# A 3x3 convolution whose output images are stored by even and by odd partitions: 32 transfers for 24

## The chip, the core and the metric

The kernel runs on one core of one Trainium2 chip. A core has five engines, each with its own instruction stream: TensorE (PE in the profile, with its weight loads as PEld), VectorE (DVE), ScalarE (ACT), GpSimd (POOL) and SyncE (SP), which here only issues DMA transfers. Sixteen DMA engines move data between the chip's memory (HBM) and the core's working memory (SBUF, 128 partitions); PSUM is the memory that TensorE writes to. The metric is the time of one execution in microseconds of device time. The kernel before takes 127.18 us, the median of three runs from 127.08 to 127.49.

## The reference

The computation is a 3x3 convolution with a border of zeros. Sixteen images of 64 channels and 64x64 points become sixteen images of 128 channels and 64x64 points, all in fp32:

```python
batch, c_in, h, w, c_out = 16, 64, 64, 64, 128
x_pad = np.pad(x, ((0, 0), (0, 0), (1, 1), (1, 1)), mode='constant')
for b in range(batch):
    for co in range(c_out):
        for ci in range(c_in):
            for kh in range(3):
                for kw in range(3):
                    output[b, co] += weight[co, ci, kh, kw] * x_pad[b, ci, kh:kh+h, kw:kw+w]
```

The input is 16.8 MB and the output 33.6 MB. Each output channel of an image is a row of 16 KB (64x64 fp32 numbers), and one image is 128 such rows, 2 MB.

## The kernel before, in words

The kernel uses a Winograd form of the convolution along the image rows: pairs of output rows are made from sums and differences of input rows, so that fewer matrix products are needed.

**Tiling.** Images go through in pairs. The 64 input channels of the first image of a pair lie on partitions 0 to 63 and those of the second on partitions 64 to 127, so one load of a pair is 128 partitions by 16 KB, 2 MB. There are eight pairs `p`, and each is worked in two halves `h` of 32 rows, so sixteen steps `(p, h)`. In a step, GpSimd makes sums, differences and outer differences of the rows in fp16 (lines 114, 121 and 127) two steps ahead, ScalarE makes an fp16 copy of 17 rows (line 132), TensorE runs 54 matrix products (line 170) into eight PSUM tiles, ScalarE copies six of them out (line 192), and VectorE (lines 247, 249, 251) and ScalarE (line 253) put the output rows together in fp32 in SBUF. In the output tiles the partition is the output channel, and every partition holds that channel's 16 KB row.

**Where the data live.** Large SBUF buffers are used more than once. Slots 0 to 4 of 16 KB for each partition, a double slot `two` for loads of pairs 3, 4, 6 and 7, and a double slot `b` for the outputs of pairs 0, 3 and 6 are handed round by the lists `X_HOME` and `O_HOME`. A tile's next user waits until the transfer that empties it has landed.

**Transfers.** All transfers are issued by SyncE, in one queue, in the order of the program. The weights and pairs 0 to 4 are loaded at the start; the loads of pairs 5, 6 and 7 follow after steps (1, 1), (3, 0) and (4, 0) (`NEXT_LOADS`, issued at line 67). Outputs of a pair are stored after its second half, by `store`. Pairs 0, 3 and 6 (`BOTH`) lie in the double slot and are stored by one transfer of 4 MB each (line 207). The other five pairs lie in two separate slots and are stored image by image (line 216). Image 11 (pair 5, second image, `FEW`) is stored in three transfers: 57 rows of all channels, then the last seven rows of 124 channels, then those of the last four channels. That makes 9 loads and 15 stores, 24 transfers.

**Completion semaphores.** The framework gives the transfers eight completion semaphores in turn. When transfer number n takes the semaphore that number n - 8 used, SyncE first waits until that earlier transfer has landed, unless something else has already made sure of it. This wait sits in SyncE's own queue, ahead of everything that SyncE issues later.

**Order.** `keep` holds the instructions of each engine in the order in which the program gives them, so nothing is rearranged by a scheduler.

Of the kernel before, what the change touches and what calls it, by code (L numbers as in the profile page):

```python
# [15 lines left out]
def kernel(  # L16
# [12 lines left out]
    nc = tc.nc  # L29
    B, CI, H, W = x.shape  # L30
    CO = weight.shape[0]
# [4 lines left out]
    keep = tc.keep_in_program_order  # L36
# [15 lines left out]
    FEW = 5, 1, 7  # L52
# [145 lines left out]
    def outputs(p):  # L198
        if O_HOME[p] == "b":
            both = slots.tile([128, 2, H, W], F32, tag="b", name="both")  # L200
            return both, [both[:, b2, :, :] for b2 in range(2)]
        return None, [home(k, "ot") for k in O_HOME[p]]

    def store(p, both, ots):
        if p in BOTH:
            pair = out[2 * p : 2 * p + 2, :, :, :].rearrange("b c h w -> c b h w")
            keep(nc.sync.dma_start(pair, both))
            return
        for b2 in range(2):
            parts = [(0, CO, 0, H)]  # L210
            if (p, b2) == FEW[:2]:
                at = H - FEW[2]
                parts = [(0, CO, 0, at), (0, 124, at, H), (124, 4, at, H)]
            for c, n, lo, hi in parts:
                keep(
                    nc.sync.dma_start(
                        out[2 * p + b2, c : c + n, lo:hi, :], ots[b2][c : c + n, lo:hi, :]
                    )
                )

    for n, (p, h) in enumerate(halves):
        if n + 2 < len(halves):
            tr[halves[n + 2]] = transforms(nc.gpsimd, *halves[n + 2])
        if h == 0:
            both, ots = outputs(p)
# [28 lines left out]
        if h == 1:  # L254
            store(p, both, ots)
# [32 lines left out]
```

## Time and profile before

| What | Value |
|---|---|
| Median of three runs | 127.18 us (127.08 to 127.49) |
| The profiled execution's own time | 127.13 us |
| Its span (first to last instruction) | 125.4 us |
| PE, DVE, ACT, POOL busy | 95.6, 66.8, 85.4, 90.5 us |
| Last output tile made by VectorE | 103.12 us |
| DMA: packets, bytes, mean rate | 3827, 50.78 MB, 405 GB/s |
| Share of the 16 DMA engines' time that is taken | 96.2% |
| Mean granted TensorE clock | 0.917 |

The profile is one execution, taken by the hardware profiler. Times in it count from the span's start. "Busy" is the time in which an engine executed something; waiting, branching and the issuing of transfers do not count. The DMA row of the page gives, for 40 equal slices of the span (3.1 us each), the mean busy share of the sixteen DMA engines in tenths, and the row below it what they moved in GB/s. Beside the views, the trace holds one record for each DMA packet: when it started, how long it took and how many bytes it moved. Data packets are mostly of 16,384 bytes, one channel's row; a packet of 4 bytes at the end of each transfer on each DMA engine is the write to the completion semaphore. The records do not name the DMA engine, but packets of one engine follow each other without a gap, so that each engine's series can be pieced together from starts and durations.

### The profile page before, as it was taken

The numbers are of one execution on the slowest core, as the hardware profiler recorded it, in microseconds if no ns is written. First come the engines' busy times: TensorE is split into PE (matmuls) and PEld (weight loads), VectorE is DVE, ScalarE is ACT, GpSimd is POOL, SyncE is SP. The second block draws the span as 40 slices with busy tenths as digits, with TensorE's granted clock in tenths as the row PEclk, the third lists the DMA queues.
The fourth block names the chain that finished last, engine by engine and source line by source line (L and its number), as shares of the span: only waits on it lengthen the run. The fifth ranks groups of instructions, "written<-read, shape, count | busy, mean of one in ns | idle before, by whom it ended". The sixth has DMA issues, their size and how long they took to land.

```text
span 125.4 us, 2343 instructions
## 1 busy us (share of the span) xinstructions
PE 95.6 (76%) x873; PEld 48.9 (39%) x873; DVE 66.8 (53%) x104; ACT 85.4 (68%) x150; POOL 90.5 (72%) x52
## 2 busy tenths in 40 slices
PE   0349999999999999999999999999999960000000
PEld 0223555555455555555555555555555520000000
DVE  0199658393939476574939394765749390000000
ACT  4458598989797988989897979789898930000000
POOL 2209999999999999999999999999999300000000
PEclk9999999999999999999999999999999996555555
DMA  4999999999999999999999999999999999999971
GB/s 132 371 453 423 434 424 439 423 335 418 434 431 429 426 434 418 423 429 434 416 439 424 423 423 423 418 431 434 423 424 423 433 416 443 423 429 444 418 335 47
DMA packets 3827, 50.78 MB, mean 405 GB/s; under 512 B 360, under 2 KB 488, under 8 KB 744
## 3 DMA queue, kind: packets, MB, share of 16 engines
q1 hardware_dynamic: 3816, 50.63, 96.2%
q8 instruction: 7, 0.11, 0.3%
q14 instruction: 4, 0.03, 0.1%
HBM read 17.07 MB, written 33.55 MB: 404 GB/s over the span
## 4 chain that ended last, share of the span: by engine, by line
PE 76%; DMA 2%; DVE 2%; POOL 1%; DVEq 0%; ACT 0%; issue 0%
PE acc L170 75%; DMA w_raw<-in_weight_dram 2%; DVE ss L114 1%; DVE ot L251 1%; POOL w L87 1%; DVEq L283 0%; DVE th L141 0%; DVE Wt L142 0%; PE wp L102 0%; ACT g0h L139 0%; DVEq L142 0%
## 5 line engine op out<-in xcount | busy, mean ns | idle before, releaser
L170 PEld LDWEIGHTS <-Wt 64*128 64x128 f16 x864 | 48.0, 96 | 48.5 <-issue 3.0
L192 ACT COPY ut<-acc 128x512 f32<-128x512 f32 x96 | 48.7, 612 | 4.4 <-PE acc L170 4.4
L170 PE MATMUL acc<-xh,Wt 64*128 64x504 f16 (+3 forms) x384 | 46.2, 372 | 0.0
L170 PE MATMUL acc<-ss,Wt 64*128 64x504 f16 (+1 forms) x192 | 24.8, 392 | 2.3 <-DVE ss L114 2.3
L170 PE MATMUL acc<-ee,Wt 64*128 64x504 f16 (+1 forms) x192 | 26.4, 377 | 0.0
L247 DVE TENSOR_TENSOR ot<-acc,ut 128x512 f32<-128x512 f32 x20 | 12.9, 686 | 20.0 <-ACT ut L192 15.8
L114 POOL TENSOR_TENSOR ss<-xs 128x1024 f16<-128x1024 f32 x7 | 16.6, 2366 | 4.7 <-DMA xs<-in_x_dram 4.7
L127 POOL TENSOR_TENSOR ee<-two 128x1024 f16<-128x1024 f32 x8 | 19.0, 2378 | 0.0
L114 POOL TENSOR_TENSOR ss<-two 128x1024 f16<-128x1024 f32 x8 | 19.0, 2369 | 0.0
L127 POOL TENSOR_TENSOR ee<-xs 128x1024 f16<-128x1024 f32 x7 | 16.6, 2376 | 0.0
L253 ACT COPY ot<-acc 128x512 f32<-128x512 f32 x20 | 10.7, 589 | 5.5 <-PE acc L170 5.5
L170 PE MATMUL acc<-dd,Wt 64*128 64x504 f16 (+1 forms) x96 | 13.9, 392 | 0.0
L247 DVE TENSOR_TENSOR both<-acc,ut 128x512 f32<-128x512 f32 x12 | 7.7, 686 | 11.0 <-ACT ut L192 7.9
L251 DVE TENSOR_TENSOR ot<-ut,acc 128x512 f32<-128x512 f32 x20 | 12.8, 682 | 0.2
L249 DVE TENSOR_TENSOR ot<-acc,ut 128x512 f32<-128x512 f32 x20 | 12.8, 680 | 0.0
L121 POOL TENSOR_TENSOR dd<-two 128x512 f16<-128x512 f32 x8 | 10.3, 1287 | 0.0
L121 POOL TENSOR_TENSOR dd<-xs 128x512 f16<-128x512 f32 x7 | 10.0, 1423 | 0.0
L132 ACT CAST xh<-two 128x1088 f16<-128x1088 f32 x8 | 9.3, 1157 | 0.0
L132 ACT CAST xh<-xs 128x1088 f16<-128x1088 f32 x8 | 9.2, 1145 | 0.0
L253 ACT COPY both<-acc 128x512 f32<-128x512 f32 x12 | 6.4, 589 | 3.5 <-PE acc L170 3.5
L251 DVE TENSOR_TENSOR both<-ut,acc 128x512 f32<-128x512 f32 x12 | 7.7, 683 | 0.1
L249 DVE TENSOR_TENSOR both<-acc,ut 128x512 f32<-128x512 f32 x12 | 7.7, 680 | 0.0
(23 smaller groups left out, 14.9 us busy)
## 6 DMA issues: line engine op xcount, KB each, us to landing
out_dram<-ot SPq DMA_DIRECT2D x9, 2048.0 KB, 18.5
out_dram<-both SPq DMA_DIRECT2D x3, 4096.0 KB, 22.5
xs<-in_x_dram SPq DMA_DIRECT2D x3, 2048.0 KB, 16.2
two<-in_x_dram SPq DMA_DIRECT2D x1, 4096.0 KB, 28.4
two<-in_x_dram SPq DMA_DIRECT2D x2, 2048.0 KB, 23.1
out_dram<-ot SPq DMA_DIRECT2D x1, 1824.0 KB, 24.3
xs<-in_x_dram SPq DMA_DIRECT2D x1, 1088.0 KB, 5.4
xs<-in_x_dram SPq DMA_DIRECT2D x1, 960.0 KB, 7.4
```

Source lines behind the costliest of these rows:

```text
L87: keep(nc.gpsimd.tensor_copy(w16[:, 0, :], w_raw))
L114: keep(eng.tensor_add(t, v[:, j : j + 16, 0, :], v[:, j : j + 16, 1, :]))
L121: keep(eng.tensor_sub(t, v[:, j : j + RB, 1, :], v[:, j : j + RB, 0, :]))
L127: keep(eng.tensor_sub(t, xs[p][:, r - 1 : r + 15, :], xs[p][:, r + 1 : r + 17, :]))
L132: keep(nc.scalar.copy(t, xs[p][:, C_ROW[h] : C_ROW[h] + 17, :]))
L170: nc.tensor.matmul(tiles[b2][:, lo:hi, c_lo:c_hi], Wt[p0 : p0 + 64, wi, kw, :], src[p0 : p0 + 64, first : last + 1 : step, c_lo + kw - 1 : ...
L192: keep(nc.scalar.copy(ut, tiles[b2]))
L247: keep(nc.vector.tensor_add(ov[b2][:, jg : jg + RB, 1, :], pg2[b2], ug[b2]))
L249: keep(nc.vector.tensor_add(ov[b2][:, jf : jf + RB, 0, :], pf1[b2], uy[b2]))
L251: keep(nc.vector.tensor_sub(ov[b2][:, jf : jf + RB, 1, :], ux[b2], pf2[b2]))
L253: keep(nc.scalar.copy(ov[b2][:, jg : jg + RB, 0, :], pg1[b2]))
```

## The change

Eight images that were stored by one transfer each are now stored by two: one takes the 64 even partitions (channels 0, 2, 4, ...), the other the 64 odd ones. The rows of 16 KB stay whole, so the number of rows and bytes moved is the same. The eight are both images of pairs 1, 2 and 4 and the first images of pairs 5 and 7. The second image of pair 5 (`FEW`) keeps its three transfers, and the second image of pair 7, the last transfer of the kernel, stays whole. Pairs 0, 3 and 6 are untouched. There are now 23 stores and 32 transfers. Line 216 of the kernel before becomes line 218. On the other engines nothing moves: the four compute engines have the same instructions in the same order.

```diff
         for b2 in range(2):
-            parts = [(0, CO, 0, H)]
+            image = out[2 * p + b2, :, :, :]
+            parts = [(slice(0, CO, 2), 0, H), (slice(1, CO, 2), 0, H)]
             if (p, b2) == FEW[:2]:
                 at = H - FEW[2]
-                parts = [(0, CO, 0, at), (0, 124, at, H), (124, 4, at, H)]
-            for c, n, lo, hi in parts:
-                keep(
-                    nc.sync.dma_start(
-                        out[2 * p + b2, c : c + n, lo:hi, :], ots[b2][c : c + n, lo:hi, :]
-                    )
-                )
+                parts = [(slice(0, CO), 0, at), (slice(0, 124), at, H), (slice(124, CO), at, H)]
+            elif p >= FEW[0] and b2 == 1:
+                parts = [(slice(0, CO), 0, H)]
+            for c, lo, hi in parts:
+                keep(nc.sync.dma_start(image[c, lo:hi, :], ots[b2][c, lo:hi, :]))
```

With the semaphores in turn, transfer n of the changed kernel waits for its own n - 8, so the pairing of transfers changes as well.

## The prediction

> **What bounds the kernel now.** I read the page from the top, then the windows of the last 25 us, then the transfers.
>
> ```profile
> PE   0349999999999999999999999999999960000000
> POOL 2209999999999999999999999999999300000000
> DMA  4999999999999999999999999999999999999971
> GB/s 132 371 453 423 434 424 439 423 335 418 434 431 429 426 434 418 423 429 434 416 439 424 423 423 423 418 431 434 423 424 423 433 416 443 423 429 444 418 335 47
> q1 hardware_dynamic: 3816, 50.63, 96.2%
> ```
>
> TensorE is full until slice 33 and then idle; the DMA engines are full from slice 2 to slice 38. The end of the time is set by transfers alone. The windows show it more closely (columns: length, busy time of PE, PEld, DVE, ACT, POOL, then clock, DMA share, GB/s):
>
> ```profile
> 90.00:100.00 10.00, 10.00 (x98) 5.14 (x94) 5.93 (x11) 8.84 (x17) 8.28 (x5) 1.00 1.00 427
> 104.00:110.00 6.00, 0.00 (x0) 0.00 (x0) 0.00 (x0) 0.00 (x0) 0.00 (x0) 0.55 1.01 431
> 110.00:120.00 10.00, 0.00 (x0) 0.00 (x0) 0.00 (x0) 0.00 (x0) 0.00 (x0) 0.50 1.01 433
> 120.00:122.00 2.00, 0.00 (x0) 0.00 (x0) 0.00 (x0) 0.00 (x0) 0.00 (x0) 0.50 0.71 303
> 122.00:124.00 2.00, 0.00 (x0) 0.00 (x0) 0.00 (x0) 0.00 (x0) 0.00 (x0) 0.50 0.21 90
> ```
>
> After 104 us no engine computes and DMA goes on at 431 to 433 GB/s; the share falls only from 120 us, when the sixteen DMA engines run out one by one. The chain of waits ends with VectorE at 103.12 us and then a wait of the closing line, so it does not name the transfers; the windows do. How far SyncE is ahead is read from the stores' view, and the tightest readers of landed data from the timelines of VectorE and GpSimd:
>
> ```profile
> DMA to landing us min/median/max: 12.0/20.6/26.6
> 82.71 1.29 DVE L247 TENSOR_TENSOR both<-acc,ut 128x512 f32<-128x512 f32 x2 [2.01 <-PE acc L170]
> 86.46 2.38 POOL L114 TENSOR_TENSOR ss<-two 128x1024 f16<-128x1024 f32 x1
> ```
>
> A 2 MB transfer takes 4.86 us of all DMA engines, so a store that lands 20.6 us after its issue stood behind some three others. The DMA queue is never short of work after 3 us. From the packet records: a 16,384-byte packet takes 611 ns and the next starts 607 ns after it, 16 x 16,384 bytes / 607 ns = 432 GB/s, the rate of the windows. The span (125.4) ends 0.83 us after the last landing at 124.52; the profiled run's own time is 127.13, so 1.73 us lie around the span, and it stands 0.05 us below the median of 127.18.
>
> **The change, part by part.**
>
> *Bytes and rows.* The same 128 rows of 16 KB for an image: no packet is cut, so nothing here at 611 ns each.
>
> *Eight more completion writes on each DMA engine.* In the records the write takes 9 ns, and a transfer of 8 packets on one engine takes 4.862 us against 8 x 607 ns = 4.856: 6 ns for the end of a transfer, no gap before the next one. The 4 MB stores say the same (9.719 us for 16 packets: 9.712 + 7). 8 x 6 ns = **0.05 us**, on the path. The Trainium skill ("DMA: Bandwidth & Descriptors", Anatomy of one DMA) gives a fixed cost of about 2 us for a transfer, mostly the wait for the write's receipt; were it paid in the queue, eight more would be an estimated 16 us. That page also says the cost can overlap, and the 6 ns here show that in this queue it does.
>
> *Eight more issues on SyncE.* An issue takes 332 to 1268 ns (median 356, stores of line 216), so 8 x 0.36 = 2.8 us, at most 10 us, over the whole run, and about 0.4 to 2.5 us at any one pair. What covers it: the data of the first split stores (issued from 34.1 us) start moving when the 4 MB store ahead of them ends, at 38.0 on the earliest DMA engine, and later ones have 5 us and more. At the end, pair 7 is issued from 103.18 in three pieces instead of two; its data start at 110.4 on the earliest engine, 7 us later. Were that cover gone, an issue would cost its own 0.36 us once for each. **0**, bounds 0 and +0.5.
>
> *Eight semaphores in turn.* Transfer n waits for n - 8, and there are now more, shorter transfers in between. I paired each with the landing of before (halves at 2.43 us). Numbering from 0, with stores ready when VectorE ended before: the load of pair 6 (number 16, ready 51.3) needs a half landed at 46.1; the 4 MB store of pair 3 (17, 57.8) needs 48.6; the load of pair 7 (18, 63.1) needs 51.0; pair 4's (19 to 22, from 68.7) need 55.8 to 63.2; pair 5's first image (23, 24, from 80.2) 65.6 and 71.5. All in time. Image 11 is the exception: its 57 rows (25) need the store of pair 3, landed at 81.28, and its seven rows (26) the load of pair 7, landed at 86.14, its last four channels (27) an even half due at about 88.6. Before, these were issued at 80.8 to 82.8; now SyncE is held until about 88.7. Queued behind it is only the 4 MB store of pair 6, ready at 92.27. And the DMA engines have work until 101.0 at the earliest (end of the 57 rows on the earliest engine), so 12 us remain. **0**; it would cost from a hold past 101 on.
>
> *Who waits for the landings.* VectorE rewrites the double slot at 82.71 and needs the store of pair 3 landed at 81.28 (1.4 us spare); GpSimd reads pair 7 at 86.46, landed at 86.14 (0.3 us spare). Both landings come after six to eight added completion writes, +0.03 to 0.04 us: still covered. If it were not, TensorE would stop, but the last stores may be issued 7 us later before DMA runs dry. **0**.
>
> *How 64 partitions are spread over the DMA engines.* This is not in the trace of before: all large transfers have 128 partitions. If each engine gets four rows of each half, its load is unchanged, but it may read partitions that another engine is reading at the same time. The nearest row is image 11's seven rows: 124 channels were moved by four DMA engines only (their completion arrives in four late steps, 103.42 to 104.19, after an early jump at issue), 31 packets of 1,792 bytes each, over all partitions that the other twelve were reading as well. All 124 took 74 ns. 1,792, 14,592 and 16,384 bytes in 74, 545 and 611 ns lie on one line (8 ns and 27.2 GB/s), and the twelve others lost nothing in these 2.2 us, bar one packet of +0.4 us beside an instruction fetch, and the disturbed engine named next, which was no slower than at other times. So **0** is nearest. Bounds: below, -0.8 (next part); above, what the one disturbed DMA engine shows: while stores ran beside computing, some 80 of its packets took about 653 instead of 611 ns; on every engine that is 8 images x 8 packets x 42 ns = +2.7 us.
> The Trainium skill ("SBUF — State Buffer", Door 1: The DMA port swizzle) has sixteen ports of about 27 GB/s, each serving eight partitions; two DMA engines on one port would get half each. The packets of 74 ns speak against it, since two engines together took some 51 GB/s there.
>
> **Sum:** 127.18 + 0.05 = 127.23, **127.2 us**. In the profile: last landing at about 124.57.
>
> **The rivals.**
>
> *Half speed (slower).* Two DMA engines share an SBUF port, or 64 partitions are given to eight engines only. Then each of the eight images takes 4.86 us more: +38.9, 166 us. For: four-engine transfers exist here, so the number of engines hangs on the shape. Against: the 74 ns packets, and 64 has room for sixteen equal shares. It decides as soon as an engine's packets in a split store take over 611 ns. Chance 0.08. Its mild form, 653 ns, gives 129.9: 0.12.
>
> *The stalls are drawn anew (slower).* The end is the latest of the sixteen DMA engines' series of packets, pieced together from the records: their last completion writes start at 124.16, 124.06, 123.37 and so on down to 120.17, mean 122.1. The latest lost 2.5 us at the first switch from loads to stores (26 to 29 us, slice 9 at 335 GB/s) and 1.1 us at 65 to 70 us, beside the load of pair 6. Single stalls of 0.35 to 0.47 us fall on other engines with instruction fetches. One more on the latest engine gives +0.4 to +0.9: 127.6 to 128.1. Chance 0.15; the runs of before, all within 0.41 us, speak against more.
>
> *The late engines are relieved (faster).* If the slow packets belong to certain partitions and not to the DMA engine, a new spread of partitions shares them out; or the 65 to 70 us stalls fall elsewhere. Then the third, 123.37, sets the end: -0.8, 126.4 us; even sharing, 122.1, would give -2.0. For: the slow series is slow in stores beside computing and clean in the loads, which looks like a path, not an engine at fault. Against: both late engines must be relieved at once. Chance 0.25.
>
> **How the numbers follow.** 0.3% (0.38 us) is about what a measurement can tell from no change. No change, 126.8 to 127.6: 0.40. Faster 0.25. Slower 0.15 + 0.12 + 0.08 = 0.35. The likeliest gives 127.2; its own range is 126.8 to 127.6. The range that leaves out no more than 2 in 10 goes from 126.2 to 129.9 and omits half speed and a gain of over 1 us.
>
> **What would show it.** Right: DMA share 9 in slices 2 to 38, 427 to 433 GB/s in the windows, the queue's share near 96%, SyncE held about 6 us longer at line 218 near 82 to 89 us, the 4 MB store of pair 6 issued near 92.3 still, no new wait of GpSimd or VectorE on a landing. Wrong: GB/s below 420 between 40 and 100 us (ports or engines shared), packets of 16,384 bytes well over 611 ns, a GpSimd wait for `two`, or a last landing below 123.8.

## The result and the profile after

The changed kernel takes 127.55 us (median of 20 runs, 127.33 to 128.29) against 127.14 us (20 runs, 126.75 to 127.66): a ratio of 1.0034, 95% interval 1.0021 to 1.0047. That is 0.41 us more, and it is just past the 0.3% that I had called the limit of what can be told.

The profiled execution took 127.45 us with a span of 125.3 us. The page after, with the lines that answer to those shown of before:

```profile
PE   0349999999999999999999999999999980000000
POOL 2209999999999999999999999999999400000000
DMA  4999999999999999999999999999999999999971
GB/s 112 392 438 434 424 455 424 418 345 418 429 434 421 431 439 413 397 424 445 421 429 413 424 434 424 434 424 431 424 424 430 410 444 427 434 424 434 439 335 58
q1 hardware_dynamic: 3944, 50.63, 96.3%
```

The DMA row is the same digit for digit, the same 50.63 MB are moved, and 128 packets more are counted: eight transfers by sixteen completion writes. The windows of the changed kernel (same columns as before):

```profile
90.00:100.00 10.00, 10.00 (x96) 5.10 (x94) 6.44 (x11) 8.68 (x17) 8.44 (x5) 1.00 1.01 429
104.00:110.00 6.00, 0.00 (x0) 0.00 (x0) 0.31 (x1) 0.00 (x0) 0.00 (x0) 0.64 0.99 423
110.00:120.00 10.00, 0.00 (x0) 0.00 (x0) 0.00 (x0) 0.00 (x0) 0.00 (x0) 0.50 1.01 433
120.00:122.00 2.00, 0.00 (x0) 0.00 (x0) 0.00 (x0) 0.00 (x0) 0.00 (x0) 0.50 0.73 311
122.00:124.00 2.00, 0.00 (x0) 0.00 (x0) 0.00 (x0) 0.00 (x0) 0.00 (x0) 0.50 0.25 107
```

The rates of these stretches are close to those of before (423 to 433 for 427 to 433 GB/s until 120 us), and DMA runs out at the same time: the last landing is at 124.48 us, before it was at 124.52. The 0.31 us of VectorE in the second line are the end of its last output tile, at 104.31 us (before, it ended at 103.72; the 103.12 in the table of the profile before is the end of the tile ahead of it).

One stretch is slower, and the prediction had named a rate below 420 GB/s between 40 and 100 us as a sign that ports or DMA engines are shared. Before:

```profile
50.00:60.00 10.00, 10.00 (x96) 5.15 (x94) 6.00 (x11) 9.12 (x18) 10.00 (x6) 1.00 1.00 426
```

and after:

```profile
50.00:60.00 10.00, 10.00 (x96) 5.10 (x94) 6.29 (x11) 8.68 (x17) 10.00 (x6) 1.00 0.99 415
```

The packet records speak against sharing: 224 of the 253 packets of 16,384 bytes in this stretch took at most 613 ns, and most of the loss lies in ten single packets of 720 to 1,186 ns from 50.2 to 52.6 us, beside the load of pair 5. The profile of the changed kernel run once more (below) has 429 GB/s in this stretch.

The view of the stores, and the two tightest readers of landed data on the timelines:

```profile
DMA to landing us min/median/max: 8.5/17.2/23.6
83.30 1.29 DVE L246 TENSOR_TENSOR both<-acc,ut 128x512 f32<-128x512 f32 x2 [2.01 <-PE acc L170]
86.66 2.34 POOL L114 TENSOR_TENSOR ss<-two 128x1024 f16<-128x1024 f32 x1
```

Nobody waits for a landing that was covered before: the store of pair 3 landed at 80.69, the load of pair 7 at 85.57.

So inside the span nothing was lost in this execution. What grew is the time around the span: the execution's own time less its span is 127.13 - 125.4 = 1.7 us before and 127.45 - 125.3 = 2.1 us after. Every run is listed with its time and, to 0.1 us, its span. Over the 20 runs of the changed kernel the mean of the difference is 2.17 us (spread 0.05), over 33 later runs of the kernel before it is 1.80 us (spread 0.04). The mean span is 125.45 us after and 125.37 us before. So of the 0.41 us some 0.36 lie outside the span, where no view of the profile shows anything.

The semaphore records of the trace go on behind the span, and they show the place. After the kernel's last instruction semaphore 2 is updated 18 times in both kernels, and in between some 250 other semaphores are updated in five blocks; no instruction of the kernel stands there. Up to the 14th of these updates, 1.69 us after the span's end, the two kernels differ by at most 2 ns. The 15th follows 0.10 us later before and 0.47 us later after, and the last three keep that distance. So 0.37 us are lost behind the last instruction, at one step of a closing sequence.

One more thing differs in the trace. The view of the line in which VectorE first writes an output tile shows, besides its 32 additions, instructions that only wait. Before:

```profile
L247 DVEq EVENT_SEMAPHORE  x35: 21/21/3206, 13.6 to 100.0; - x35
```

and after:

```profile
L246 DVEq EVENT_SEMAPHORE  x40: 21/21/3206, 14.2 to 100.5; - x40
```

A tile that was emptied by one transfer waits for one completion semaphore before it is written again. A tile that was emptied by two waits for two, and the trace has five more waiting instructions for it. In all it has 179 instructions on VectorE before and 184 after. Most of the waiting instructions take 21 ns (the median), on an engine that is not the bound.

### The profile page after: what moved, and what is told of

Read it like the earlier page. It is cut to its first block, busy times and chain, and to the rows that moved or that the text cites. A ratio compares the mean times of both kernels' runs of the same rounds, so it can differ in the third digit from the quotient of the medians.

```text
span 125.3 us, 2356 instructions
## 1 busy us (share of the span) xinstructions
PE 96.1 (77%) x873; PEld 48.7 (39%) x873; DVE 66.9 (53%) x104; ACT 85.4 (68%) x150; POOL 90.5 (72%) x52
## 3 DMA queue, kind: packets, MB, share of 16 engines
q1 hardware_dynamic: 3944, 50.63, 96.3%
## 4 chain that ended last, share of the span: by engine, by line
PE 76%; DMA 2%; DVE 2%; POOL 1%; DVEq 0%; ACT 0%; issue 0%
PE acc L170 76%; DMA w_raw<-in_weight_dram 2%; DVE ss L114 1%; DVE ot L250 1%; POOL w L87 1%; DVEq L282 0%; DVE th L141 0%; DVE Wt L142 0%; PE wp L102 0%; ACT g0h L139 0%; DVEq L142 0%
## 5 line engine op out<-in xcount | busy, mean ns | idle before, releaser
L170 PE MATMUL acc<-xh,Wt 64*128 64x504 f16 (+3 forms) x384 | 46.7, 375 | 0.0
```

The source lines that it names most:

```text
L170: nc.tensor.matmul(tiles[b2][:, lo:hi, c_lo:c_hi], Wt[p0 : p0 + 64, wi, kw, :], src[p0 : p0 + 64, first : last + 1 : step, c_lo + kw - 1 : ...
```

## The experiments

All comparisons are with runs of the kernel before on the same chip. "Around" is the mean of time less span, over the runs.

| Kernel | Transfers | VectorE instructions | Median, us (before) | Ratio, 95% interval | Mean span (before) | Around |
|---|---|---|---|---|---|---|
| before | 24 | 179 | 127.09 | | 125.37 | 1.80 |
| eight tiny loads | 32 | 179 | 127.35 (127.09) | 1.0021 (0.9997 to 1.0045) | 125.58 (125.37) | 1.81 |
| rows instead of partitions | 32 | 184 | 127.85 (127.09) | 1.0058 (1.0034 to 1.0081) | 125.81 (125.37) | 2.17 |
| four images only | 28 | 183 | 127.96 (127.09) | 1.0069 (1.0040 to 1.0097) | 125.87 (125.37) | 2.14 |
| quarters | 48 | 188 | 127.79 (127.09) | 1.0050 (1.0032 to 1.0069) | 125.87 (125.37) | 2.01 |
| before, 5 on VectorE | 24 | 184 | 127.38 (127.18) | 1.0015 (0.9996 to 1.0035) | 125.27 (125.40) | 2.19 |
| before, 5 on ScalarE | 24 | 179 | 127.13 (127.18) | 1.0001 (0.9984 to 1.0019) | 125.37 (125.40) | 1.83 |
| before, 12 on VectorE | 24 | 191 | 127.19 (127.18) | 1.0002 (0.9983 to 1.0021) | 125.32 (125.40) | 1.95 |
| change, 12 on VectorE | 32 | 196 | 127.71 (127.18) | 1.0043 (1.0022 to 1.0065) | 125.90 (125.40) | 1.82 |
| before, 2 on VectorE | 24 | 181 | 127.18 (127.07) | 1.0001 (0.9985 to 1.0018) | 125.33 (125.35) | 1.82 |
| change, 20 on VectorE | 32 | 204 | 127.26 (127.07) | 1.0008 (0.9989 to 1.0027) | 125.54 (125.35) | 1.79 |
| change, once more | 32 | 184 | 127.62 (127.07) | 1.0036 (1.0018 to 1.0055) | 125.49 (125.35) | 2.16 |

### Is it the number of transfers? Eight tiny loads

```diff
+    spare = const.tile([16, 8, 64], F32)
+    spares = iter(range(8))
...
+            if p < FEW[0] or b2 == 0:
+                k = next(spares)
+                keep(nc.sync.dma_start(spare[:, k, :], x[0, 0:16, k, :]))
```

> The kernel before, with its eight images stored whole, and eight tiny loads added (16 partitions by 256 bytes each, into a tile that nothing reads), one behind each of the eight stores: 32 transfers, each on sixteen DMA engines. In the profiles the span did not grow with the change (125.4 to 125.3 us) while the time around the span did, from 1.7 to 2.1 us. Theory A, each transfer costs about 0.05 us outside the span whatever it moves: outside 2.1, in all about +0.4 to +0.5 us (0.36 outside, and at most 8 x 25 ns = 0.2 inside). Theory B, the shape with 64 partitions costs it: outside 1.7, in all 0 to +0.2 us.

Around the span 1.81: the 32 transfers cost nothing there. This was my first theory and it fell. The mean span grew by 0.2 us, which is the bound, but with a standard error of 0.13 us this is not clear of the noise. In the trace SyncE has 61 instructions, as many as in the change, so the length of its program is not the cause either.

### Is it the shape? Rows instead of partitions

```diff
-            parts = [(slice(0, CO, 2), 0, H), (slice(1, CO, 2), 0, H)]
+            parts = [(slice(0, CO), 0, 32), (slice(0, CO), 32, H)]
```

> The same eight images in two transfers each, cut by rows instead of partitions: 128 partitions by 8 KB, so twice the packets for these images and 32 transfers. Inside the span, a packet has about 8 ns beside its bytes, so 8 images x 8 more packets x 8 ns = +0.5 us, and 0.05 for the completions. Theory A: outside 2.1, in all +0.9 us. Theory B (64 partitions): outside 1.7, in all +0.55. A third, C, each packet costs outside the span: the change adds 8 completion packets for each DMA engine, this kernel 72, so outside about 1.7 + 9 x 0.36 = 5 us.

Around 2.17 with all 128 partitions in every transfer, so it is not the 64 partitions; and not 5 us, so it is not the packets. The in-all figure came out near theory A's (+0.76 for +0.9), but the tiny loads had already excluded A. Inside the span the terms of the prediction hold: +0.44 us for an expected 0.55.

### Half the change

```diff
-            elif p >= FEW[0] and b2 == 1:
+            elif p >= 4:
                 parts = [(slice(0, CO), 0, H)]
```

> Only the four images of pairs 1 and 2 are stored by even and odd partitions: 28 transfers. Theory A: half of the cost, outside 1.9, in all +0.2 us. B: the same here. A theory D, a step that comes with a program of a certain length, gives 1.7 or 2.1 and nothing between.

Around 2.14, nearly the whole step for half of the images. This is not the 1.9 of theories A and B; of the three, only a step (theory D) fits it. The span is a surprise, +0.50 us with fewer transfers than in the change. Its windows show where (same columns as above; the last two are DMA share and GB/s):

```profile
60.00:64.00 4.00, 4.00 (x42) 2.05 (x38) 3.19 (x6) 3.34 (x7) 4.00 (x3) 1.00 0.99 416
64.00:68.00 4.00, 4.00 (x42) 2.04 (x38) 2.83 (x5) 3.56 (x7) 4.00 (x3) 1.00 1.01 365
68.00:72.00 4.00, 4.00 (x41) 1.94 (x37) 1.99 (x4) 3.78 (x8) 4.00 (x3) 1.00 1.01 430
```

Between 64 and 68 us, while the load of pair 6 goes through, DMA falls to 365 GB/s. By the packet records the 16,384-byte packets from 60 to 72 us took 11.1 us of DMA-engine time beyond 611 ns each, against 3.0 us before. Why this profile shows it and the others do not was not settled.

### Quarters

```diff
-            parts = [(slice(0, CO, 2), 0, H), (slice(1, CO, 2), 0, H)]
+            parts = [(slice(k, CO, 4), 0, H) for k in range(4)]
```

> The same eight images in four transfers each, every fourth partition: 48 transfers, sixteen DMA engines with two rows each. Inside the span +24 x 6 ns = 0.15 us, and SyncE held longer by its semaphores, with DMA still supplied. Theory A: outside 1.7 + 24 x 0.045 = 2.8 us, in all +1.2 us. Theory D (a step): outside 2.1, in all +0.5 us. If the two sets of partitions meet on a port, the packets get longer than 611 ns here more than in the change.

Around 2.01, less than in the change with 24 transfers more than before: no cost for each transfer. Packets did not get longer: 2121 of 2261 packets of 16,384 bytes after 30 us took at most 613 ns, against 2090 of 2260 before. So every fourth partition runs at full rate too. The span is +0.5 us, 0.35 more than its terms; its profile has packets disturbed as the prediction described (94 of 625 to 680 ns, against 91 before), but whether they lie on the DMA engine that ends last the records do not settle. At this point one thing in the traces set the kernel at 1.81 apart from those above 2.0: it has 179 instructions on VectorE, they have 183 to 188. The next two runs test that.

### Five instructions on VectorE, nothing else

```diff
+    spare = const.tile([128, 5], F32)
+    spares = iter(range(5))
...
+        k = next(spares, None)
+        if k is not None:
+            keep(nc.vector.tensor_copy(spare[:, k : k + 1], th[:, k : k + 1]))
         if h == 1:
             store(p, both, ots)
```

> The kernel before with its 24 transfers, and five copies of one column (128x1 elements) added on VectorE in the first five steps, into a tile that nothing reads. In the traces the change has five more waiting instructions on VectorE (184 for 179), since a tile that was stored by two transfers waits for two semaphores before it is rewritten; the kernel with eight tiny loads has 179 and its time around the span was 1.81, as before. Theory E, the time around the span hangs on the number of VectorE's instructions: 184 here, outside 2.17 as in the change, span as before, in all +0.35 us. Theory F, it is the waits for transfers or the split stores themselves: outside 1.80, in all 0.

Around 2.19, with whole stores and 24 transfers. Theory F is out. Nothing else of the change is in this kernel; the added work is five copies of 147 ns, done by 40 us:

```profile
L259 DVE COPY spare<-th x5: 145/147/147, 17.0 to 40.0; 128x1 f32<-128x1 f32 x5
```

Its mean span is 0.12 us below that of before, so the ratio alone (1.0015, interval across 1) would not have shown it; time less span, with a spread of 0.05 us, does.

### The same five on ScalarE

```diff
-            keep(nc.vector.tensor_copy(spare[:, k : k + 1], th[:, k : k + 1]))
+            keep(nc.scalar.copy(spare[:, k : k + 1], g0h[:, k : k + 1]))
```

> The kernel before with five copies of one column added on ScalarE instead (259 instructions for 254; VectorE 179). Theory E: outside 1.80, in all 0 to +0.1. Theory G, any engine's longer program costs it: outside about 2.0 to 2.2. The kernel in quarters had 259 on ScalarE and 188 on VectorE, and 2.0.

Around 1.83. So five instructions more on ScalarE cost nothing there, and eight more on SyncE cost nothing in the kernel with tiny loads (1.81); five more on VectorE do. GpSimd and TensorE were not tried.

### More of them, with and without the split

The same edit on VectorE with twelve copies, on the change and on the kernel before.

> The changed kernel with twelve such copies more on VectorE (196 instructions). If the time around the span grows with the length, outside is above 2.17 (by 0.07 for each instruction it would be 3.0). If it depends on where the program's end falls against blocks in which instructions are fetched, it is anything from 1.7 to 2.3 and not in proportion; a value near 1.8 would make this kernel as fast as before, about 127.2 us.

> The kernel before with twelve copies on VectorE (191 instructions). Theory E: as its number of VectorE instructions says, between the kernels with 184 and 196, whether the stores are split or not. Theory F: outside 1.80.

With the split stores and 196 instructions the time around the span is back at 1.82; with whole stores and 191 it is 1.95. So the split alone does not bring the cost, the number on VectorE does, and not in proportion. The first kernel is still no faster than the change, since its span grew to 125.90. The packets of the instruction queue tell something of this. All kernels with at most 184 instructions have four packets of 8,192 bytes on it after the span's start, from 34 to 85 us. The kernel with 196 has a fifth at 105.2 us:

```profile
q14 instruction: 5, 0.04, 0.1%
```

In its records the DMA engine that ends last has one packet 0.35 us longer at 105.6 us, just behind it. The kernel with 191 has its fifth at 126.2 us, 1.1 us after the end of its span, and the one in quarters (188, and five more on ScalarE) has two at 127.5 and 127.6 us, 1.7 and 1.8 us after the end of its own.

### Two and twenty, and the change once more

Again the same edit, with two copies on the kernel before and with twenty on the change (two in each of the first four steps, then one), and the change unaltered.

> The kernel before with two copies of one column added on VectorE (181 instructions). So far the time around the span is 1.80 to 1.83 at 179, 2.14 at 183, 2.17 to 2.19 at 184, 1.95 at 191 and 1.82 at 196: a step up somewhere from 180 to 183, then down by about 0.03 us for each instruction. Theory E as a fetch of instructions after a block boundary: 1.81 here if the boundary lies past 181, about 2.25 if it lies before.

> The changed kernel with twenty copies of one column on VectorE (204 instructions). Theory E: the boundary is passed well inside the span, outside 1.8. With twelve copies the fetch fell at 105.2 us and held up one packet of the latest DMA engine by 0.35 us; here it comes earlier, while there is still computing. Span 125.4 as in the change, in all about 127.2, level with before, if the fetch does not fall on the latest engine again; 127.6 if it does.

> The changed kernel once more, unaltered, beside the same chip's runs of the kernel before: span of all runs +0.05 to +0.1 us by the completion writes, around the span +0.36 us, in all +0.4 us. If the cost around the span belonged to one chip or day, it would be 1.8 here.

At 181 still 1.82, so the step lies at 182 or 183. At 204, with the split in place, 1.79, and the fifth packet comes at 103.8 us; this kernel, the change with twenty useless instructions added, takes 127.26 us and is faster than the change (127.62, same chip), level with before. The change run once more has 2.16 and an excess of half a microsecond (0.55 us by the medians, 0.50 by the means of span and time around it), so the cost belongs to the program and not to a day or chip. No kernel here is faster than the kernel before.

**What is shown and what is argued.** Shown: the time around the span is 1.79 to 1.83 us for 179, 181, 196 and 204 instructions on VectorE, and 2.14 to 2.19 for 183 and 184, with and without split stores; it falls between, 2.01 at 188 and 1.95 at 191.

Shown too, by the semaphore records behind the span, is that the place of the loss moves with this number:

| VectorE instructions | Where the closing sequence is late |
|---|---|
| 179, 181, 196, 204 | nowhere; the step from the 14th to the 15th update takes 0.10 us, the last update comes 1.90 to 1.91 us after the span's end |
| 183 | nowhere up to the last update, 1.91 us after the span's end, though the profiled execution has 2.12 us around the span: outside what the records show |
| 184 (all four profiles) | in the step from the 14th update, 1.7 to 1.8 us after the span's end, to the 15th: 0.47 to 0.48 us for 0.10 |
| 188 (quarters) | in two of the five blocks, due 0.66 and 0.78 us after the span's end: 0.41 and 0.52 us late |
| 191 | in the step from the third update, 0.47 us after the span's end, to the fourth: 0.19 us for 0.04 |

From 184 on, the longer VectorE's program is, the earlier the loss comes, until at 196 and 204 there is none behind the span. The kernel in quarters is not a clean case: it also has five more instructions on ScalarE and 23 more on SyncE, and two late blocks and two packets where the kernel with 191 has one late step and one packet.

Argued: that this is the crossing from one fetched block of VectorE's instructions to the next, which falls into the closing sequence when the kernel's part ends shortly before it, into the span when that part is longer, and is not reached when it is shorter. The packets at 105.2 and 103.8 us for 196 and 204, inside the span, and those behind the span for 188 and 191 fit it. That VectorE waits for such a packet to land does not fit: with 191 the late step is over 0.66 us after the span's end and the packet starts at 1.10, with 188 the second late block starts at 1.30 and the packets at 1.68 and 1.80. At 183 and 184 no fifth packet is in the records at all. So what the engine does in the 0.37 us stays open. The Trainium skill ("Runtime: NRT & Kernel Launch", Instruction fetch mechanics) says that an engine's instructions are fetched in blocks ahead of execution and that crossing a block boundary is mostly hidden. The traces have such packets, but of 8,192 bytes on this queue where the page has blocks of 16 KiB; and if the crossing is the cause, up to 0.38 us are not hidden here.

## Why the prediction was right or wrong

**The bound.** Right: transfers alone set the end of the span, at the same rates but for the ten microseconds from 50 us on, and the last DMA engine ends at 124.14 us for 124.16.

**Completion writes, 0.05 us.** Not contradicted, and too small to be confirmed: the mean span is +0.08 us over the first runs, +0.14 us in the repeat and +0.19 with the twenty copies, each with a standard error of 0.08 or 0.09 us.

**Issues on SyncE.** Nothing on the path, as said. Issues were dearer than the median that I took (628 for 356 ns; up to four now come in a row), but covered.

**Semaphores in turn.** Right. Image 11's last two transfers were issued at 85.58 and 88.03 us (said: about 86.1 and 88.7), and the 4 MB store of pair 6 at 92.86, with no harm. SyncE's waits show the two holds:

```profile
SPq L218 <- DMA two<-in_x_dram: 2.4, 1, 2.4
SPq L218 <- DMA out_dram<-ot: 2.1, 1, 2.1
```

**64 partitions.** Right: each half's completion climbs in sixteen late steps, so sixteen DMA engines carry it, and 2114 of 2258 packets of 16,384 bytes after 30 us took at most 613 ns. Reading 74 ns off the seven-row packets of image 11 was the right row. By the rule that the prediction drew from the Trainium skill ("SBUF — State Buffer", Door 1: The DMA port swizzle) the packets would, by its estimate, have gone at half speed if two engines met on a port; nothing of that appears, in halves or in quarters. Whether two engines did meet there no record shows.

**Who waits for the landings, 0.** No engine waits longer, as the prediction said. (Only four added completion writes stand ahead of the two landings, not six to eight; the pair 4 stores come behind them. That is 0.02 us and changes nothing.) But here its account has a gap: I asked only when the landings come and not what waiting for two of them takes on the waiting engine, which is five more instructions on VectorE. The chapter on the change even says that the four compute engines have the same instructions; that is true of their operations and false of their waits.

**The time around the span.** This is the term that the prediction had wrong. I put 1.73 us there and carried it over unchanged in the sum, so at 0 for the change, without a reason. It grew by 0.36 us, and this is all of the difference that is clear of noise.

**The rivals.** The measured 127.55 lies in the range and just inside the likeliest case's own range (126.8 to 127.6), but that is luck: the sum said 127.23, the difference comes from a term that no rival named, and only the width of the range took it in. "Slower" had 0.35, for other reasons. Half speed and its mild form did not happen. Stalls drawn anew did: in the profile after, the engine that ends last, at 124.14, is one of the four that carry image 11's seven rows; before, the one that ended last was not. Yet the end stayed, and no one was relieved. Slow stalls of that kind are the likelier reading of the half-microsecond spans of three experiments (four images only, quarters, twelve copies on the change), but that was seen in profiles, one each, and not tested.

## What to carry to other kernels

Compare the time less the span, before and after, ahead of any search inside the span: here it varied by 0.04 to 0.07 us from run to run while the total varied by 0.2 to 0.4, and with the five copies it found a third of a microsecond that the total's interval hid. The semaphore records behind the span then show at which step it is lost. Splitting a transfer also splits the wait of whoever uses the buffer next, so count waiting instructions on every engine, not only the transfers. Where a kernel's gains are parts of a per cent, the length of an engine's program is itself a variable, and a padded control (a few instructions whose result nobody reads, nothing else) is a way to see it.

## What the runs showed of the hardware that I had not expected

- Five copies of one column on VectorE, done by 40 us, cost 0.38 us after the kernel's last instruction, at 125 us; two cost nothing, and twenty on the changed kernel took its excess away again.
- Eight more transfers of sixteen 256-byte rows added 0.2 us (standard error 0.13) to the mean span, data packets and completion writes together, and nothing around it: in this queue, which is kept full, a transfer more cost about 25 ns at the end.
- A 16,384-byte packet takes 611 ns (the median) whether the transfer covers every, every second or every fourth partition.
